# A quarter of the weights' low parts computed on GpSimd instead of VectorE, in a seven-phase transformer kernel

## The chip, the cores and the metric

The kernel runs on one core of one Trainium2 chip. The metric is the device time of one execution in microseconds (us), the median of three runs. The engines are called as the profile calls them: PE (TensorE, matmuls) with PEld (its weight loads), DVE (VectorE), ACT (ScalarE), POOL (GpSimd), SP (SyncE, which here only issues DMAs).

## What is computed

Two blocks run one after the other on x of 256 tokens by 1024 features, all in float32. The first has two layers: RMS norm, a projection to q, k, v and a gate, rotary embedding, attention (a sliding window with sinks in layer a, causal attention in layer b), the gate, an output projection, a residual. The second has two layers of a hybrid mixer (attention and a Mamba-2 scan side by side) and a SwiGLU:

```python
h = h + hybrid_mixer(rmsnorm_2(h, norm_mix[layer]), w_in[layer], ...)
h = h + swiglu(rmsnorm_2(h, norm_ffn[layer]), w_gate[layer], w_up[layer], w_down[layer])
...
def swiglu(h, w_gate, w_up, w_down):
    return (jax.nn.silu(h @ w_gate) * (h @ w_up)) @ w_down
```

Every weight matrix is read once from HBM: 140 MB in all.

## The kernel before

**Phases.** The names of tiles begin with the phase: `a`, `b` (the attention layers' projections), `m` (the mixers, twice), `f` (the SwiGLU's gate and up projections, twice), and with an `o` behind (`ao`, `bo`, `mo`, `fo`) the output projection of each. In the traced execution the matmuls of a run about from 3 to 81 us, ao to 107, b to 179, bo to 209, the first m to 316, mo to 355, the first f to 478, fo to 539, the second m to 643, mo to 680, f to 800, fo to the end.

**Three products for one.** A float32 product is made of three matmuls in the faster type fp32r. Each weight tile of 128 x 512 (two k tiles of 256 columns) is taken apart in `feed` (L362): `hi` is the raw weight rounded to fp32r, a copy on ACT or DVE (L392 to L395), and `lo` is `raw - hi`, a subtraction on DVE (L396). The activations are split likewise into `xh` and `xl`. `emit_slot` (L423) then issues hi by xh, hi by xl and lo by xh into one PSUM bank; in f the first two are one matmul of 512 columns. So each `lo` is needed by PE a little behind its `hi`. A sum of 526 such subtractions stands on DVE.

**The order is fixed when the program is built.** Each engine has its own queue, in order, and an instruction waits on semaphores for what it reads and for the buffer that it writes. The order in the queues comes from a planner within the kernel: `account` (L251) keeps for every engine a clock `clk` of when it would be done, `cost` (L223) gives the ns that an instruction is put down for, and `run_plan` (L487) calls in turn `feed` (next weights), `step_sides` (all that is not a weight matmul: attention, scan, norms, gates, each a chain that is resumed when PE's clock passes the end of its last step) and `emit_slot` (the next k tile's matmuls). `feed` runs ahead of PE by at most 60 k tiles (LEAD), and only while neither DVE's nor ACT's clock is over 500 ns ahead of PE's (AHEAD), unless the tile is needed within 5 (URGENT). It chooses the engine of the `hi` copy by the two clocks (L392). Other places choose by them too: `scaled` (ACT or DVE, whichever would be done first) and `spare`.

**Buffers.** Raw weights land by DMA from SP's queue in three buffers of 8 k tiles (`wraw`, RAW) or in pages; a buffer is loaded anew when its last `hi` and `lo` are done. `hi` and `lo` are pages of a pool of 64.

**POOL before.** It runs twelve powers of -1/2 of 128 x 2 numbers (the norms' reciprocal roots, in `columns` and `final`) and a few small fills, each put down at 650 ns by the planner.

Of the kernel before, what the change touches and what calls it, by code (L numbers as in the profile page):

```python
# [11 lines left out]
F32 = mybir.dt.float32  # L12
# [52 lines left out]
class Engine:  # L65


    def __init__(self, build, name, real):
        self.build, self.ename, self.real = build, name, real
# [43 lines left out]
class Build:  # L113
# [38 lines left out]
    def __init__(self, ctx, tc, io):  # L152
        self.tc = tc
        self.nc = Engines(self, tc.nc)
        self.clk = dict(PE=0.0, DVE=0.0, ACT=0.0, POOL=0.0)
        self.cur = Chain(None, 0.0)
        self.cur.start = 0.0
        self.count = 0
        self.io = io
        self.n = 0  # L160
        self.phase = "i"

        def pool(name, bufs, **kw):
            return ctx.enter_context(tc.tile_pool(name=name, bufs=bufs, **kw))

        self.cp = pool("const", 1)
        self.wraw = pool("wraw", self.RAW)
        self.fp = pool("f", self.PAGES)
        self.xp = pool("x", 4)
        self.up = pool("u", 2)  # L170
        self.hp = pool("h", 6)
        self.sp = pool("s", 8)
        psum = dict(space=bass.MemoryType.PSUM)
        self.pp = pool("psum", 8, **psum)
        self.banks = [0.0] * 8
        self.used = dict(mm=0, sc=0, tr=0, pv=0, out=0)
        self.sides = []
        self.ups = self.raws = 0
        self.planned = {}
        self.landing = 0.0  # L180
        self.live = self.wlive = self.most = 0
        self.kept = {}
        self.x = Timed(self)
        self.res = Timed(self)
        self.plan = []
        self.dma_i = self.cast_i = self.cast_k = self.cast_slot = 0
        self.seg_i = self.seg_k = self.seg_m = self.slot = 0
        self.dma_at = 1200.0
        self.queue = self.nc.sync
        self.units = {}  # L190
        self.bubbles = {}


    def name(self, s):
# [28 lines left out]
    def cost(self, eng, op, args, kw):  # L223
        out = kw.get("out", args[0] if args else None)
        aps = [x for x in list(args) + list(kw.values()) if hasattr(x, "shape")]
        n = 1
        for d in out.shape[1:]:
            n *= d
        cols = sum(1 for x in aps if x is not out and len(x.shape) == 2 and x.shape[1] == 1 and n > 1)
        psum = any("PSUM" in str(getattr(getattr(x, "tensor", x), "space", "")) for x in aps)  # L230
        if eng == "PE":
            if op == "transpose":
                return 110.0
            f32 = args[1].dtype == F32
            if args[1].dtype == BF16:
                return 69.0 if n == 128 else n / 2.4 * 1.02
            if f32 and out.shape[0] == 64:
                return 0.95 * n
            if n < 128:
                return 110.0 * (2 if f32 else 1)  # L240
            return n / 2.4 * (4 if f32 else 1) * 1.02
        if eng == "ACT":
            acc = "accum_out" in kw
            return (52.0 if psum else 93.0) + 0.833 * n + 93.0 * cols
        if eng == "POOL":
            return 650.0
        if op in ("tensor_copy", "tensor_scalar") and not psum:
            return 68.0 + 0.52 * n + 93.0 * cols
        return (130.0 if psum else 68.0) + 1.042 * n + 93.0 * (cols if op != "tensor_tensor_reduce" else 0)
# [112 lines left out]
    def feed(self):  # L362

        nc = self.nc
        while self.dma_i < len(self.plan) and self.raws < self.RAW:
            self.feed_dma()
        while self.cast_i < self.dma_i and self.cast_slot < self.slot + self.LEAD:
            now = self.clk["PE"]
            urgent = self.cast_slot < self.slot + self.URGENT
            if not urgent and max(self.clk["DVE"], self.clk["ACT"]) > now + self.AHEAD:  # L370
                return
            s = self.plan[self.cast_i]
            if s["at"] > now:
                self.landing = s["at"]
                return
            k = s["k0"] + self.cast_k
            n = min(2, s["k1"] - k)
            if self.wlive >= self.WMIN and self.wlive + self.live + self.SPARE > self.PAGES:
                return
            self.wlive += 2  # L380
            raw = s["raw"][:, self.cast_k:self.cast_k + n, :]
            hi = self.fp.tile([P, n, S], F32R, tag="f", name=self.name("hi"))
            if s["mode"] == "dt":

                both = hi[:, :, 0:32]
                raw, hi, lo = raw[:, :, 0:16], both[:, :, 0:16], both[:, :, 16:32]
            else:
                lo = self.fp.tile([P, n, S], F32R, tag="f", name=self.name("lo"))
            at = s["at"]
            self.cur = Chain(None, at)  # L390
            self.cur.start = at
            if self.clk["DVE"] + self.SWAP < self.clk["ACT"]:  # L392
                nc.vector.tensor_copy(hi, raw)
            else:
                nc.scalar.activation(hi, raw, AF.Copy)  # L395
            nc.vector.tensor_sub(lo, raw, hi.bitcast(F32))  # L396
            for i in range(n):
                s["parts"][k + i] = ((both if s["mode"] == "dt" else hi)[:, i, :], lo[:, i, :], self.cur.ready)
            self.cast_k += n
            self.cast_slot += n  # L400
            if s["k0"] + self.cast_k == s["k1"]:
                self.cast_i += 1
                self.cast_k = 0
                if s["page"]:
                    self.drop()
                else:
                    self.raws -= 1
# [1317 lines left out]
```

## Time and profile before

| | |
|---|---|
| median of 3 runs | 883.34 us (882.36 to 884.08) |
| the profiled execution | 882.25 us |
| its span, from first to last instruction | 880.2 us |
| busy: PE, DVE, ACT, POOL | 865.3, 731.8, 556.8, 14.6 us |
| matmuls recorded | 6451 |
| read from HBM | 140.15 MB |
| PE's granted clock, mean | 0.997 of full speed |

The profile is of one execution. "Busy" is the time in which at least one instruction of an engine was under way; matmuls overlap, so a busy PE is not PE at its peak. The times in the views count from the span's start.

### The profile page before, as it was taken

To read this page: it belongs to the slowest core of one execution; us is meant where nothing else is said; L and a number is where in the kernel's file an instruction comes from. 1 tells how busy PE (TensorE), PEld (TensorE's weight loads), DVE (VectorE), ACT (ScalarE), POOL (GpSimd) and SP (SyncE) were. 2 spreads that over 40 slices of the span, in tenths; PEclk is the share of its full clock that TensorE was granted. 3 is DMA by queue.
4 is the path that set the end of the run, shared out by engine and by line. 5 is a ranking of instruction groups with operands and counts; after the bars stand their busy time and mean duration, and the time that the engine had idled before them with its cause. 6 is when DMAs were issued, how large, how long until landed. Compare 5 with 4: busy or idle time off the path is not lost.

```text
span 880.2 us, 16862 instructions
## 1 busy us (share of the span) xinstructions
PE 865.3 (98%) x6451; PEld 793.9 (90%) x6451; DVE 731.8 (83%) x1652; ACT 556.8 (63%) x1325; POOL 14.6 (2%) x30
## 2 busy tenths in 40 slices
PE   8999999999999999999999999999999999999996
PEld 7987999889999789888888889999899888889996
DVE  6999899998899998899988668889878898998431
ACT  6378763677688885666666445579655666666321
POOL 0000010000000000000000000000000000000000
PEclk9999999999999999999999999999999999999998
DMA  8512673035543046666655637420046665665401
GB/s 315 206 74 73 225 275 130 26 107 177 199 145 108 26 132 215 200 226 224 234 207 179 234 127 274 158 73 25 2 137 217 224 229 200 240 220 187 167 1 48
DMA packets 30385, 142.30 MB, mean 162 GB/s; under 512 B 5344, under 2 KB 6880, under 8 KB 18400
## 3 DMA queue, kind: packets, MB, share of 16 engines
q1 hardware_dynamic: 30016, 141.08, 46.8%
q8 instruction: 51, 0.84, 0.4%
q14 instruction: 30, 0.25, 0.1%
q10 hardware_dynamic: 288, 0.14, 0.1%
HBM read 140.15 MB, written 1.05 MB: 160 GB/s over the span
## 4 chain that ended last, share of the span: by engine, by line
PE 66%; issue 21%; DVE 6%; ACT 4%; DMA 2%; SPq 0%; POOL 0%; POOLq 0%; DVEq 0%
PE m__p L78 20%; PE f__p L78 15%; PE mo__p L78 9%; PE b__p L78 8%; PE fo__p L78 7%; PE bo__p L78 3%; PE ao__p L78 3%; PE a__p L78 1%; DVE a__lo L78 1%; DVE a__sm L78 1%; ACT m__m L78 1%; DMA cst<-cst 1%; DMA fo__raw<-wa 1%; DVE a__pe L78 1%; DVE a__rope L78 1%
## 5 line engine op out<-in xcount | busy, mean ns | idle before, releaser
L78 PE MATMUL f__p<-mo__x,f__hi 128*128 128x512 f32 x492 | 174.6, 396 | 0.0
L78 DVE TENSOR_TENSOR f__lo<-f__raw,f__hi 128x512 fp32r<-128x512 f32 x186 | 123.0, 687 | 21.7 <-ACT f__hi L78 21.1
L78 PE MATMUL f__p<-mo__x,f__lo 128*128 128x256 f32 x492 | 138.0, 280 | 0.0
L78 PEld LDWEIGHTS f__p<-mo__x,f__hi 128*128 128x128 f32 x492 | 92.3, 188 | 21.5
L78 ACT ACTIVATE f__hi<-f__raw 128x512 fp32r<-128x512 f32 x186 | 104.6, 621 | 0.0
L78 PEld LDWEIGHTS f__p<-mo__x,f__lo 128*128 128x128 f32 x492 | 93.0, 189 | 0.0
L78 PE MATMUL fo__p<-f__r,fo__hi 128*128 128x256 f32 (+1 forms) x308 | 74.1, 322 | 0.0
L78 ACT ACTIVATE f__sum<-f__p 128x256 f32<-128x256 f32 x84 | 29.8, 383 | 56.8 <-PE f__p L78 56.7
L78 PE MATMUL f__p<-f__x,f__hi 128*128 128x512 f32 x176 | 63.6, 395 | 0.0
L78 DVE TENSOR_TENSOR m__lo<-m__raw,m__hi 128x512 fp32r<-128x512 f32 x74 | 50.2, 687 | 11.8 <-ACT m__hi L78 11.1
L78 PE MATMUL fo__p<-f__r,fo__lo 128*128 128x256 f32 x208 | 58.5, 281 | 0.0
L78 PEld LDWEIGHTS fo__p<-f__r,fo__hi 128*128 128x128 f32 x308 | 51.4, 190 | 4.4
L78 PE MATMUL m__p<-bo__x,m__hi 128*128 128x256 f32 (+1 forms) x292 | 54.2, 287 | 0.5 <-ACT m__m L78 0.5
L78 PE MATMUL mo__p<-mo__r,mo__hi 128*128 128x256 f32 x288 | 52.5, 284 | 0.0
L78 PE MATMUL a__p<-fo__x,a__hi 128*128 128x256 f32 x272 | 50.8, 287 | 0.7 <-ACT a__hi L78 0.7
L78 PE MATMUL f__p<-f__x,f__lo 128*128 128x256 f32 x176 | 49.3, 280 | 0.0
L78 DVE TENSOR_TENSOR fo__lo<-fo__raw,fo__hi 128x512 fp32r<-128x512 f32 (+1 forms) x60 | 37.3, 669 | 11.9 <-ACT fo__hi L78 9.3
L78 PEld LDWEIGHTS m__p<-bo__x,m__hi 128*128 128x128 f32 (+1 forms) x292 | 44.8, 188 | 2.4 <-issue 1.3
L78 PEld LDWEIGHTS mo__p<-mo__r,mo__hi 128*128 128x128 f32 x288 | 44.8, 192 | 0.2 <-issue 0.2
L78 ACT ACTIVATE m__hi<-m__raw 128x512 fp32r<-128x512 f32 x66 | 40.0, 635 | 7.3 <-DMA m__raw<-w 7.3
L78 PEld LDWEIGHTS a__p<-fo__x,a__hi 128*128 128x128 f32 x272 | 42.1, 191 | 2.1 <-ACT a__hi L78 1.3
L78 ACT ACTIVATE fo__hi<-fo__raw 128x512 fp32r<-128x512 f32 (+2 forms) x61 | 31.7, 580 | 17.4 <-DMA fo__raw<-w 10.0
(540 smaller groups left out, 2465.0 us busy)
## 6 DMA issues: line engine op xcount, KB each, us to landing
f__raw<-wu SPq DMA_DIRECT2D x20, 1024.0 KB, 4.8
f__raw<-wg SPq DMA_DIRECT2D x19, 1024.0 KB, 4.8
m__raw<-w SPq DMA_DIRECT2D x17, 1024.0 KB, 4.8
f__raw<-wd SPq DMA_DIRECT2D x9, 1024.0 KB, 4.9
b__raw<-wb SPq DMA_DIRECT2D x7, 1024.0 KB, 6.4
fo__raw<-wd SPq DMA_DIRECT2D x7, 1024.0 KB, 4.9
mo__raw<-wo SPq DMA_DIRECT2D x12, 512.0 KB, 3.7
fo__raw<-w SPq DMA_DIRECT2D x5, 1024.0 KB, 4.9
```

The lines of the kernel that those rows point to most:

```text
L78: return fn(*args, **kw)
```

## The change

In `feed`, the subtraction that makes `lo` may now go to POOL. The planner works out when DVE and when POOL would finish it, from the later of the engine's clock and the time when the `hi` copy is done, and takes POOL where that is no later than DVE (never for the small tiles of mode "dt"). `cost` puts down a POOL instruction of 64 elements or more at 100 + 2.3 ns for each element, 1278 ns for the usual 512. `share` only counts.

```diff
@@ -243,7 +244,7 @@
         if eng == "POOL":
-            return 650.0
+            return 650.0 if n < 64 else 100.0 + 2.3 * n
...
@@ -393,7 +394,12 @@
             else:
                 nc.scalar.activation(hi, raw, AF.Copy)
-            nc.vector.tensor_sub(lo, raw, hi.bitcast(F32))
+
+            t = max(t for t in self.cur.last.values())
+            late = [max(t, self.clk[e]) + self.cost(e, "tensor_sub", (lo, raw), {}) for e in ("DVE", "POOL")]
+            sub = nc.gpsimd if late[1] <= late[0] and s["mode"] != "dt" else nc.vector
+            sub.tensor_sub(lo, raw, hi.bitcast(F32))
+            self.share[sub is nc.gpsimd] += 1
```

In the built program 132 of the 526 subtractions stand on POOL: 12 in a (one of them half as long), 3 in ao, 17 in b, 2 in bo, 13 and 6 in the two m, 4 and 5 in the two mo, 30 and 31 in the two f, 6 and 3 in the two fo. Since the planner's clocks now run differently, its other choices move too: 11 `hi` copies, 23 scalings and taps of the mixers and the attention go from ACT to DVE (DVE has 34 such instructions more and 4 additions of 512 elements less, ACT 46 less). PE has as many instructions as before, interleaved a little differently.

The first place is POOL's queue around the norm of layer b. The rows are `lo` subtractions and the powers, `b__s<-b__s,mhalf`. Before:

```order
L78 TENSOR_TENSOR a__s_387<-a__s_385,mhalf 128x2
L78 TENSOR_TENSOR b__s_1773<-b__s_1771,mhalf 128x2
L78 TENSOR_TENSOR m__s_3310<-m__s_3308,mhalf 128x2
L78 TENSOR_TENSOR m__s_3346<-m__s_3306,mhalf 128x2
L78 MEMSET m__u_3424 128x2x3
```

Now:

```order
L78 TENSOR_TENSOR b__lo_1709<-ao__raw_1557,b__hi_1708 128x512
L78 TENSOR_TENSOR b__lo_1713<-ao__raw_1557,b__hi_1712 128x512
L78 TENSOR_TENSOR b__lo_1773<-ao__raw_1590,b__hi_1772 128x512
L78 TENSOR_TENSOR b__lo_1781<-ao__raw_1633,b__hi_1780 128x512
L78 TENSOR_TENSOR b__s_1805<-b__s_1803,mhalf 128x2
L78 TENSOR_TENSOR b__lo_1921<-b__raw_1797,b__hi_1920 128x512
L78 TENSOR_TENSOR b__lo_1973<-b__raw_1823,b__hi_1972 128x512
```

The norm's power stands behind four subtractions of the same phase; before, it had nothing but the last norm's power ahead of it.

The second place is DVE's queue late in the second f, twelve rows up to the product of a unit with its gate (`f__sum<-f__p` adds the two halves of a PSUM bank, `f__rowh` and `f__row` are the norm's factors, `f__gt` the gate). Before:

```order
L78 TENSOR_TENSOR f__lo_10594<-f__raw_10463,f__hi_10593 128x512
L78 TENSOR_TENSOR f__lo_10605<-f__raw_10463,f__hi_10604 128x512
L78 SCALAR_TENSOR_TENSOR f__gt_10575<-f__gt_10575,f__sum_10544 128x512
L78 TENSOR_TENSOR f__lo_10621<-f__raw_10463,f__hi_10620 128x512
L78 TENSOR_TENSOR f__sum_10609<-f__p_10533,f__sum_10609 128x256
L78 TENSOR_TENSOR f__sum_10609<-f__p_10534,f__sum_10609 128x256
L78 TENSOR_TENSOR f__lo_10637<-f__raw_10514,f__hi_10636 128x512
L78 TENSOR_TENSOR f__lo_10645<-f__raw_10514,f__hi_10644 128x512
L78 TENSOR_TENSOR f__sum_10609<-f__sum_10609,f__row_9574 128x512
L78 TENSOR_TENSOR f__lo_10658<-f__raw_10514,f__hi_10657 128x512
L78 TENSOR_TENSOR f__lo_10668<-f__raw_10514,f__hi_10667 128x512
L78 TENSOR_TENSOR f__sum_10609<-f__sum_10609,f__gt_10575 128x512
```

Now, up to the same step:

```order
L78 TENSOR_TENSOR f__sum_10666<-f__p_10597,f__sum_10666 128x256
L78 TENSOR_TENSOR f__sum_10666<-f__p_10598,f__sum_10666 128x256
L78 TENSOR_TENSOR f__sum_10666<-f__sum_10666,f__rowh_9568 128x512
L78 SCALAR_TENSOR_TENSOR f__gt_10679<-f__gt_10679,f__sum_10666 128x512
L78 TENSOR_TENSOR f__lo_10700<-f__raw_10500,f__hi_10699 128x512
L78 TENSOR_TENSOR f__lo_10714<-f__raw_10574,f__hi_10713 128x512
L78 CAST f__hi_10730<-f__raw_10574 128x512
L78 TENSOR_TENSOR f__lo_10731<-f__raw_10574,f__hi_10730 128x512
L78 TENSOR_TENSOR f__sum_10723<-f__p_10660,f__sum_10723 128x256
L78 TENSOR_TENSOR f__sum_10723<-f__p_10661,f__sum_10723 128x256
L78 TENSOR_TENSOR f__sum_10723<-f__sum_10723,f__row_9566 128x512
L78 TENSOR_TENSOR f__sum_10723<-f__sum_10723,f__gt_10679 128x512
```

POOL's queue about there:

```order
L78 TENSOR_TENSOR f__lo_10566<-f__raw_10363,f__hi_10565 128x512
L78 TENSOR_TENSOR f__lo_10626<-f__raw_10426,f__hi_10625 128x512
L78 TENSOR_TENSOR f__lo_10686<-f__raw_10500,f__hi_10685 128x512
L78 TENSOR_TENSOR f__lo_10746<-f__raw_10574,f__hi_10745 128x512
L78 TENSOR_TENSOR f__lo_10806<-f__raw_10634,f__hi_10805 128x512
```

Of seven subtractions in twelve rows of DVE three are left, beside a `hi` copy that has come from ACT; the unit's own additions and products stand closer together, and POOL does a subtraction or two for every four `lo` that a raw buffer of 8 k tiles gives.

## Rows read from the trace of the kernel before

**Rows 1.** The page, part 1: busy time of each engine, its share of the span, instructions.

```profile
PE 865.3 (98%) x6451; PEld 793.9 (90%) x6451; DVE 731.8 (83%) x1652; ACT 556.8 (63%) x1325; POOL 14.6 (2%) x30
```

**Rows 2.** Busy time of each engine in nine stretches of the span.

```profile
core 0: us, PE busy (x) PEld busy (x) DVE busy (x) ACT busy (x) POOL busy (x), PEclk, DMA share, GB/s
...
0.00:20.00 20.00, 15.99 (x111) 13.89 (x111) 11.37 (x26) 13.06 (x30) 0.34 (x6) 1.00 0.86 306
...
33.00:81.00 48.00, 47.10 (x394) 40.88 (x392) 46.99 (x154) 30.80 (x104) 0.00 (x0) 1.00 0.25 89
...
107.00:179.00 72.00, 72.00 (x607) 67.37 (x605) 66.44 (x182) 41.41 (x102) 2.79 (x1) 1.00 0.41 143
...
209.00:268.00 59.00, 59.00 (x493) 58.63 (x492) 53.65 (x125) 40.85 (x90) 2.19 (x8) 1.00 0.53 180
...
268.00:316.00 48.00, 46.69 (x418) 40.60 (x418) 45.06 (x121) 44.70 (x145) 0.00 (x0) 1.00 0.18 56
...
355.00:478.00 123.00, 123.00 (x714) 108.40 (x713) 110.37 (x212) 79.34 (x173) 0.69 (x1) 1.00 0.62 216
...
680.00:800.00 120.00, 120.00 (x685) 104.18 (x684) 109.30 (x200) 77.80 (x161) 1.07 (x1) 1.00 0.64 221
...
800.00:880.00 80.00, 72.33 (x589) 71.10 (x587) 31.66 (x54) 26.15 (x51) 0.69 (x1) 0.97 0.26 90
```

**Rows 3.** Chain of work that ended last, in order of time: its longest piece.

```profile
691.80 181.25 issue
```

**Rows 4.** Timeline, DVE and PE: first low part of a stage, and its first matmul.

```profile
107.19 0.69 DVE L78 TENSOR_TENSOR b__lo<-ao__raw,b__hi 128x512 fp32r<-128x512 f32 x1
...
114.32 0.28 PE L78 MATMUL b__p<-b__x,b__lo 128*128 128x256 f32 x1
...
355.89 0.69 DVE L78 TENSOR_TENSOR f__lo<-mo__raw,f__hi 128x512 fp32r<-128x512 f32 x1 [0.63 <-ACT f__hi L78]
...
362.18 0.28 PE L78 MATMUL f__p<-f__x,f__lo 128*128 128x256 f32 x1
...
682.33 0.68 DVE L78 TENSOR_TENSOR f__lo<-mo__raw,f__hi 128x512 fp32r<-128x512 f32 x1
...
686.17 0.28 PE L78 MATMUL f__p<-mo__x,f__lo 128*128 128x256 f32 x1
```

**Rows 5.** Timeline of DVE beside three powers on GpSimd, and a CAST: start, length.

```profile
115.64 2.49 DVE L78 TENSOR_TENSOR b__lo<-b__raw,b__hi 128x512 fp32r<-128x512 f32 x4
...
221.02 1.89 DVE L78 TENSOR_TENSOR m__lo<-m__raw,m__hi 128x512 fp32r<-128x512 f32 x3
...
365.17 0.75 DVE L78 TENSOR_TENSOR f__sum<-f__p,f__sum 128x256 f32<-128x256 f32 x2
...
599.91 0.42 DVE L78 CAST m__hi<-m__raw 128x512 fp32r<-128x512 f32 x1
```

**Rows 6.** Timeline of GpSimd (POOL): four of its twelve powers.

```profile
115.90 2.79 POOL L78 TENSOR_TENSOR b__s<-b__s,mhalf 128x2 f32<-128x2 f32 x1 [91.00 <-ACT b__hi L78]
...
221.25 1.00 POOL L78 TENSOR_TENSOR m__s<-m__s,mhalf 128x2 f32<-128x2 f32 x1 [102.57 <-DVE m__s L78]
...
223.55 0.69 POOL L78 TENSOR_TENSOR m__s<-m__s,mhalf 128x2 f32<-128x2 f32 x1 [1.30 <-PE m__p L78]
...
365.33 0.69 POOL L78 TENSOR_TENSOR f__s<-f__s,mhalf 128x2 f32<-128x2 f32 x1 [30.73 <-DVE f__s L78]
```

**Rows 7.** Busy time of instructions on PSUM tiles alone; columns of rows 2 without POOL.

```profile
33.00:81.00 48.00, 43.35 (x362) 37.95 (x360) 18.58 (x42) 5.74 (x12) 1.00 0.25 89
...
209.00:268.00 59.00, 58.91 (x490) 58.63 (x491) 8.32 (x20) 1.73 (x4) 1.00 0.53 180
...
268.00:316.00 48.00, 41.84 (x379) 34.52 (x346) 13.10 (x32) 19.47 (x70) 1.00 0.18 56
...
355.00:478.00 123.00, 123.00 (x712) 108.27 (x711) 16.48 (x45) 14.71 (x42) 1.00 0.62 216
```

More of the change, by code (lines that the diff above doesn't have):

```diff
@@ L191, in __init__ @@
         self.bubbles = {}
+        self.share = [0, 0]
     def name(self, s):
```

## The prediction

> **What bounds the kernel.** I read the busy times of the page first: PE is busy for 865.3 us of a span of 880.2, DVE for 731.8, POOL for 14.6 [rows 1]. So all that another engine could give back is 14.9 us. The same by stages shows where they lie [rows 2]: 4.0 us in the first 20 (loads; PE has 15.99), 7.7 in the last 80 (the tail behind the last matmul; 72.33), hence 3.2 in all the rest. Of these, 0.9 are in 33 to 81, where DVE is busy for 46.99 of 48 us and sets the pace, and 1.3 in 268 to 316, where DVE (45.06) and ACT (44.70) take turns. In b (107 to 179) and both f (355 to 478, 680 to 800) PE is busy throughout, though DVE is at 90% there. The chain of waits says it from the other side: its longest piece, 181.25 us from 691.80 on, is PE's own issue with no wait for anyone [rows 3]. The change does not touch PE's work: as many matmuls, as many columns. **It can give 3.2 us at most, and the question is what it can cost.**
>
> A cost needs the low parts to come late. How early they come now, the first subtraction of a stage and the first matmul that reads it show [rows 4]: in b it ends at 107.19 + 0.69 = 107.88, its matmul starts at 114.32, a lead of 6.4 us; in the first f 356.58 against 362.18, 5.6; in the second f 683.01 against 686.17, 3.2. These leads are all that stands between a slower DVE and PE.
>
> **What is removed.** 132 subtractions leave DVE. Four in a row take 2.49 us and one 0.69 [rows 4, 5], so each holds the queue for (2.49 - 0.69) / 3 = 0.60 us: 79 us less on DVE. On the other side the planner, which sees DVE lighter, gives it 34 copies and scalings more and 4 additions less; at 0.42 us (a CAST [rows 5]) and 0.69 that is 34 x 0.42 - 4 x 0.69 = 11.5 us, of which I count 2.5 in each f (six copies) and 4 in the first m. ACT sheds 46 instructions; it is the bound nowhere but between 268 and 316, so I give that nothing.
>
> **What is added, and its two unknowns.** POOL gets 132 subtractions of 512 elements. No row shows one. Its shortest instruction with two inputs, a power of two elements, takes 0.69 us, the longest 2.79 [rows 6]; those are the bounds of the time. I take 1.28, the planner's own figure for 512 elements in the diff, about twice what DVE needs.
>
> The second unknown is what DVE does meanwhile, and here the trace speaks. The same power takes 0.69 us at 223.55, when DVE does nothing, and 0.69 at 365.33, when DVE adds from a PSUM bank (`f__sum<-f__p`). It takes 1.00 at 221.25 beside DVE's subtractions, and 2.79 at 115.90: it ended at 118.69, so its 0.69 us began at 118.0, when the four subtractions that DVE had begun at 115.64 were done [rows 5, 6]. POOL waits while DVE works from SBUF alone, and not while DVE reads PSUM. The POOL instructions of before read next to nothing, so no row shows the reverse; I take it that the way is held by whoever came first, that a POOL subtraction holds it for all its 1.28 us, and that DVE's SBUF work stands still. The bounds are 0 (DVE feels nothing) and 2.79 us.
>
> [...]
>
> So a moved subtraction costs DVE q x 1.28 - 0.60 us, where q is the share of DVE's time without PSUM. From DVE's time on PSUM tiles and from its busy time by stage [rows 2, 7] q is 1 - 18.58 / 46.99 = 0.60 in 33 to 81, 1 - (8.32 + 13.10) / (53.65 + 45.06) = 0.78 in the first m (209 to 316), 1 - 16.48 / 110.37 = 0.85 in f. For the first 33 us and b I take 0.78.
>
> - **a**: five of its twelve go in the first 33 us, 5 x 0.40 = 2.0 us, seven after, 7 x 0.17 = 1.2. DVE has nothing spare there: **+3**.
> - **b**: 17 x 0.40 and four copies at 0.42 are 8.5 us on top of 66.44 in a stage of 72. 2.9 too many, but the lead is 6.4: **0**. POOL's queue now has subtractions ahead of the norm's power. That it came 2.1 us late at 115.90 cost PE nothing (72.00 of 72), and one more wait of 1.28 I put at 0 too.
> - **first m**: 13 x 0.40 + 4 = 9.2 on top of 98.71 in 107: 0.9 too many, **+1**.
> - **first f**: 30 x 0.49 + 2.5 = 17.2 on top of 110.37: 127.6 in a stage of 123. Over by 4.6, with a lead of 5.6, which DVE's waits for PE and ACT use up in part: **+1.5**.
> - **second f**: 31 x 0.49 + 2.5 = 17.7 on top of 109.30: 127.0 in 120. Over by 7.0, lead 3.2; part of the work is for the next stage and may come late: **+3**.
> - ao, bo, both mo, the second m and both fo have 29 between them, and more room: **0**. DMAs: SP's next load into a raw buffer waits for POOL's subtraction as it did for DVE's; there are three buffers, and the transfers keep their lead as long as the `lo` keep theirs, so 0.
>
> Sum: 3 + 1 + 1.5 + 3 = 8.5 us on the profiled execution's 882.25, 890.8. The median of the runs is 1.1 above that execution, so **892**.
>
> [...]
>
> **The rivals.** Under 0.2% (1.8 us) a measurement of this kernel can't tell a change from none.
>
> - *The leads swallow all.* DVE is over its stages only by what the buffered leads hold, and a's 3 us shrink since PE there lacks 0.9. For: the overrun in the first f is smaller than its lead. Against: the second f. It gives 883.3, within 0.2%.
> - *DVE feels nothing* (or POOL's hold is under 0.60 / 0.78 = 0.77 us, from where each moved subtraction relieves DVE). It turns the sign: DVE loses 12 x 0.60 = 7.2 us in a, where it sets the pace, 7.8 in the first m, and PE fills its 3.2 us there. For: no row shows DVE waiting for POOL. Against: POOL waits for DVE, and one way for two engines is most simply exclusive. 882.25 - 3.2 + 1.1 = 880.2, faster.
> - *Each change of hands costs as well.* The power of 1.00 us shows 0.31 of waiting beside running subtractions; if DVE loses that much on top, the hold is 1.59 and a moved subtraction costs 0.75 in f. First f 135.4 in 123, less the lead, 6.8; second f 135.1 in 120, 11.9; first m 4.5; a 5.7: 29 in all, 912.
>
> That the change does not do what it says is no case: the queues as built hold the 132.
>
> **How the numbers follow.** Chances: forecast 0.44, leads swallow all 0.22, DVE feels nothing 0.23, changes of hands 0.11. The forecast's own range is 886 to 901 (one stage's term doubled, or the f terms gone). Over all cases I say 879 to 906: it takes in the gain of 3 us with one more for the interleaving, and leaves out the last rival and a little of the rest. Faster by over 0.2%: the third case less a bit whose gain is under 1.8 us, 0.22. Slower: forecast and last rival, 0.55. Within: 0.23.
>
> **What would show it.** Right: DVE's SBUF instructions beside a POOL subtraction take up to 1.3 us longer or begin that much later, PSUM ones do not; POOL's subtractions take 1.1 to 1.4 us when alone; the leads at the end of f are gone, and PE's idle time before `lo` matmuls in a and the second f names POOL or DVE. Wrong: DVE's subtractions keep 0.69 us beside POOL's, or DVE's total busy time falls by some 68 us (79 less 11.5) while PE's idle time is as before.

## The result and the profile after

| | before | after |
|---|---|---|
| median of 5 runs | 882.78 us (882.36 to 884.08) | 927.53 us (920.84 to 928.72) |
| the profiled execution, its span | 882.25, 880.2 us | 920.84, 919.1 us |
| PE's granted clock, mean | 0.997 | 0.987 |

The ratio is 1.049 (1.046 to 1.052): 44.7 us slower, outside the range of 879 to 906. The profiled execution is the fastest of the five; the other four have a mean granted clock of 0.978 to 0.983.

Part 1 of the page of after, the answer to [rows 1]:

```profile
PE 878.2 (96%) x6451; PEld 801.4 (87%) x6451; DVE 773.6 (84%) x1550; ACT 538.1 (59%) x1279; POOL 206.5 (22%) x162
```

DVE has 102 instructions fewer and is busy 41.8 us longer. Where that comes from is in the groups by line, shape and tile of after (count, busy us, mean ns):

```profile
L78 DVE TENSOR_TENSOR f__lo<-f__raw,f__hi 128x512 fp32r<-128x512 f32 x122 | 99.0, 838 | 3.1 <-ACT f__hi L78 0.7 <-PE f__p L78 0.5
L78 DVE TENSOR_TENSOR f__sum<-f__p,f__sum 128x256 f32<-128x256 f32 x84 | 31.4, 414 | 0.0
L78 DVE TENSOR_TENSOR f__sum<-f__sum,f__rowh 128x512 f32<-128x512 f32 x22 | 30.0, 1364 | 0.4
```

Before, their means were 687, 417 and 685 ns. What reads a PSUM bank (`f__p`) is as it was, what works from SBUF alone takes longer, the product with `f__rowh` twice as long. The timelines of POOL and of DVE in one place of the first f show why (start, length):

```profile
442.44 1.30 POOL L78 TENSOR_TENSOR f__lo<-f__raw,f__hi 128x512 fp32r<-128x512 f32 x1 [3.40 <-ACT f__hi L78]
...
442.63 1.66 DVE L78 TENSOR_TENSOR f__lo<-f__raw,f__hi 128x512 fp32r<-128x512 f32 x1
444.21 0.41 DVE L78 TENSOR_TENSOR f__sum<-f__p,f__sum 128x256 f32<-128x256 f32 x1
```

DVE's subtraction starts 0.19 us behind POOL's and ends at 444.29, 0.55 us after POOL's end at 443.74. It takes 0.97 us longer than its usual 0.69, and most of those 0.69 lie behind POOL's end: it stood still until POOL was done. Of the 1177 DVE instructions that touch no PSUM tile (names in `__p`) 117 are over 0.1 us longer than the median of their operation and shape before, together 105.0 us, the longest by 1.14; of the 373 that touch one, none. So the hold is 105.0 / 132 = 0.80 us for each moved subtraction. Below, "hold" is such stretch of DVE's instructions, in sum; the runs without GpSimd's subtractions give it as a difference of DVE's busy time too.

The low parts do not come late. The answer to [rows 4] in b, timelines of DVE and PE:

```profile
113.64 0.69 DVE L78 TENSOR_TENSOR b__lo<-ao__raw,b__hi 128x512 fp32r<-128x512 f32 x1
...
131.87 0.28 PE L78 MATMUL b__p<-ao__x,b__lo 128*128 128x256 f32 x1
```

The lead is 131.87 - 114.33 = 17.5 us; it was 6.4. In the two f the first `lo` and the first matmul that reads one are (timelines of POOL, DVE and PE):

```profile
376.52 1.75 POOL L78 TENSOR_TENSOR f__lo<-mo__raw,f__hi 128x512 fp32r<-128x512 f32 x1
...
389.55 0.28 PE L78 MATMUL f__p<-f__x,f__lo 128*128 128x256 f32 x1
...
713.98 0.69 DVE L78 TENSOR_TENSOR f__lo<-mo__raw,f__hi 128x512 fp32r<-128x512 f32 x1 [0.63 <-ACT f__hi L78]
...
722.79 0.28 PE L78 MATMUL f__p<-mo__x,f__lo 128*128 128x256 f32 x1
```

These leads are 11.3 us (before 5.6) and 8.1 us (before 3.2). PE waits for DVE's other steps. All its waits in the trace come to 33.4 us, before to 7.7, and none of after's is put down to a `hi` or a `lo`. The 25.7 us more of waits and PE's busy time, 12.9 us longer, make up nearly all of the 38.9 us by which the span grew. The two longest waits are for a rotary product in b and for the last residual. Timelines of PE, of DVE, and of PE again:

```profile
166.07 0.28 PE L78 MATMUL b__p<-ao__x,b__lo 128*128 128x256 f32 x1
171.02 1.22 PE L78 MATMUL b__p<-b__rope,b__rope 64*128 64x128 f32 x6 [4.66 <-DVE b__rope L78]
...
169.20 1.76 DVE L78 TENSOR_TENSOR b__rope<-b__rope,b__rot 128x512 f32<-128x512 f32 x1
...
861.38 1.30 PE L78 MATMUL fo__p<-cst,fo__hg 128*128 128x128 f32 x4 [4.38 <-ACT fo__hg L78]
```

What PE was late for at 861.38 the chain of waits follows back, in order of time (start, length):

```profile
846.15 0.69 DVE f__lo L78
846.83 0.35 DVE fo__hi L78
847.21 1.72 DVE fo__lo L78
848.92 0.68 DVE fo__sum L78 x2
849.62 0.70 DVE fo__sum L78
850.35 0.70 DVE fo__sum L78
...
851.13 0.64 ACT fo__r L78
851.79 0.55 DVE fo__r L78
...
852.40 0.69 DVE fo__lo L78
...
853.15 5.08 DMA fo__raw<-wd
...
858.31 0.64 ACT fo__hi L78
858.98 0.69 DVE fo__lo L78
859.67 0.61 DVE fo__h L78
860.30 0.63 ACT fo__sq L78
860.93 0.41 ACT fo__hg L78
```

DVE is behind; its `fo__lo` of 852.40 frees a raw buffer late, the load into it lands at 858.23, and the residual `fo__h`, which does not need that weight, stands in DVE's queue behind the `lo` that does. The chain into the rotary product of 171.02 runs through late loads as well, each behind a `lo` of DVE:

```profile
125.85 0.61 DVE b__lo L78
...
126.51 6.55 DMA b__raw<-wb
...
149.04 1.21 DVE b__lo L78 x2
150.27 4.74 DMA b__raw<-wo
```

For the whole span the chain is now PE 49%, DVE 29%, DMA 8% (before PE 66%, DVE 6%, DMA 2%).

PE's granted clock is lower too. Three stretches of after, the last inside the first (columns of [rows 2]):

```profile
160.00:180.00 20.00, 15.34 (x111) 13.88 (x110) 19.48 (x53) 6.79 (x17) 4.05 (x3) 0.83 0.28 96
846.00:866.00 20.00, 13.63 (x96) 12.77 (x96) 16.78 (x27) 11.21 (x22) 2.55 (x2) 0.91 0.68 230
...
169.00:175.00 6.00, 3.98 (x19) 3.33 (x20) 6.00 (x9) 2.77 (x4) 3.08 (x2) 0.50 0.21 78
```

DVE is busy for 19.48 of the 20 us around the wait in b. Within that wait the clock falls: from 168.6 on PE is granted 0.50, for 6.8 us.

### The profile page after: what moved, and what is told of

Its sections match the earlier page's. It is cut to its first block, busy times and chain, and to the rows that moved or that the text cites. A ratio compares the mean times of both kernels' runs of the same rounds, so it can differ in the third digit from the quotient of the medians.

```text
span 919.1 us, 17113 instructions
## 1 busy us (share of the span) xinstructions
PE 878.2 (96%) x6451; PEld 801.4 (87%) x6451; DVE 773.6 (84%) x1550; ACT 538.1 (59%) x1279; POOL 206.5 (22%) x162
## 4 chain that ended last, share of the span: by engine, by line
PE 49%; DVE 29%; DMA 8%; issue 8%; ACT 6%; SPq 0%; POOL 0%; DVEq 0%; POOLq 0%; ACTq 0%
PE f__p L78 19%; PE m__p L78 16%; PE fo__p L78 6%; DVE f__sum L78 3%; DVE f__lo L78 3%; PE bo__p L78 3%; PE b__p L78 3%; DVE mo__lo L78 2%; PE a__p L78 2%; DVE b__lo L78 1%; DVE m__xs L78 1%; DVE m__lo L78 1%; DMA mo__raw<-wg 1%; DMA mo__raw<-wo 1%; DVE a__lo L78 1%
## 5 line engine op out<-in xcount | busy, mean ns | idle before, releaser
L78 PE MATMUL f__p<-mo__x,f__hi 128*128 128x512 f32 x400 | 142.2, 396 | 0.0
L78 PE MATMUL f__p<-mo__x,f__lo 128*128 128x256 f32 x400 | 112.2, 281 | 0.0
L78 POOL TENSOR_TENSOR f__lo<-f__raw,f__hi 128x512 fp32r<-128x512 f32 x54 | 75.1, 1397 | 163.8 <-ACT f__hi L78 114.1
L78 DVE TENSOR_TENSOR f__lo<-f__raw,f__hi 128x512 fp32r<-128x512 f32 x122 | 99.0, 838 | 3.1 <-ACT f__hi L78 0.7
L78 PE MATMUL f__p<-f__x,f__hi 128*128 128x512 f32 x244 | 87.0, 393 | 0.0
L78 PE MATMUL f__p<-f__x,f__lo 128*128 128x256 f32 x244 | 68.4, 280 | 0.0
L78 PEld LDWEIGHTS f__p<-f__x,f__hi 128*128 128x128 f32 x244 | 45.7, 187 | 10.5
L78 PEld LDWEIGHTS f__p<-f__x,f__lo 128*128 128x128 f32 x244 | 46.1, 189 | 0.0
L78 DVE TENSOR_TENSOR fo__lo<-fo__raw,fo__hi 128x512 fp32r<-128x512 f32 (+1 forms) x49 | 31.7, 692 | 15.8 <-ACT fo__hi L78 12.9
L78 PE MATMUL fo__p<-f__r,f__hi 128*128 128x256 f32 (+1 forms) x180 | 43.8, 326 | 0.0
L78 DVE TENSOR_TENSOR m__lo<-m__raw,m__hi 128x512 fp32r<-128x512 f32 x48 | 32.5, 688 | 11.0 <-ACT m__hi L78 10.6
```

The costliest lines, as they stand in the source:

```text
L78: return fn(*args, **kw)
```

## The experiments

In every diff `tc.nc` issues without telling the planner (unbooked), `nc` books; `MOVED` is a constant with a bit for each subtraction that the change puts on GpSimd, `moved()` in these cuts a test of it. "Place" is one of these 132. All times are medians; the kernel before ran beside them at 882.1 to 882.6.

**1. What holds DVE.** The order of before, and at the places GpSimd work that nobody needs. (A copy reads `raw` alone, so it starts when the load lands and not, as a subtraction does, when `hi` is done.)

```diff
             nc.vector.tensor_sub(lo, raw, hi.bitcast(F32))
+            if moved():
+                tc.nc.gpsimd.tensor_sub(junk, raw, hi)       # e2
+                tc.nc.gpsimd.tensor_sub(tiny, raw[:, 0, 0:2], hi[:, 0, 0:2])   # e3
+                tc.nc.gpsimd.memset(junk, ...)               # e3, twice
+                tc.nc.gpsimd.tensor_copy(junk, raw)          # e8
```

> The order of the kernel before with all subtractions on DVE; at the 132 places GpSimd repeats the subtraction into a scratch tile that nobody reads, and the planner does not know of it. Nothing waits for GpSimd's results. Theory (a GpSimd subtraction holds DVE's SBUF work by 0.8 us on average): DVE busy 731.8 + about 100 = 830 us, and more loss than the change since nothing leaves DVE: 930 to 980 us. If the change's loss came of its order or of GpSimd's results coming late: 883, DVE busy 732.

> As the run before it, but at the 132 places GpSimd does a subtraction of two elements (which only keeps the place in time) and two fills of 128 x 512, which write SBUF and read nothing. It tells what of a GpSimd instruction holds DVE. If only reading from SBUF holds: DVE's subtractions keep 0.69 us, DVE busy 732 to 760, 883 to 890 us. If any use of SBUF by GpSimd holds, writes too: DVE busy over 800 and a loss as with the repeated subtractions, in proportion to the fills' length (a fill's length no trace shows).

> The order of the kernel before, all subtractions on DVE; at the 132 places GpSimd copies raw (128x512, one input) into a scratch tile, unbooked. It tells whether GpSimd's reading from SBUF with one input holds DVE as the subtraction with two did (841 us busy on DVE, 950 us), or not, as the fills did (734, 884). If any reading holds, in proportion to the copy's length (no row shows it; by the fill at least 0.53 us): DVE busy 780 to 840 us and 915 to 950 us. If only two inputs hold: 883 to 886.

Measured: subtractions 950.09 us, DVE busy 841.1; fills 883.81, DVE 734.2; copies 882.77, DVE 759.3. DVE's subtractions in f, and POOL's work beside them, from the groups by line and shape; with subtractions:

```profile
L78 DVE TENSOR_TENSOR f__lo<-f__raw,f__hi 128x512 fp32r<-128x512 f32 x186 | 147.2, 816 | 10.1 <-ACT f__hi L78 9.0
```

With fills:

```profile
L405 POOL MEMSET junk<- 128x512 f32 x132 | 70.0, 530 | 7.6
...
L78 DVE TENSOR_TENSOR f__lo<-f__raw,f__hi 128x512 fp32r<-128x512 f32 x186 | 123.0, 686 | 22.6 <-ACT f__hi L78 21.6
```

With copies:

```profile
L78 DVE TENSOR_TENSOR f__lo<-f__raw,f__hi 128x512 fp32r<-128x512 f32 x186 | 131.8, 734 | 8.3 <-ACT f__hi L78 7.6
```

So GpSimd's reading holds DVE's subtractions (816 ns beside subtractions, 734 beside copies) and its writing does not: fills leave 686 ns, where before has 687, although there are 264 of 0.53 us. A copy (0.64 us at 444.81 in e8, with one input) holds for 27.5 / 132 = 0.21 us, a subtraction (1.29 us alone) for 109.3 / 132 = 0.83 us; how much of the difference comes of the copies' other start is not shown.

Fills do hold a few other DVE instructions, with one input of full size: in their run 12 TENSOR_SCALAR and one CAST are 0.14 to 0.48 us longer than the median before, 4.0 us in all. Timelines of DVE and of POOL:

```profile
295.70 0.85 DVE L78 CAST m__hi<-m__raw 128x512 fp32r<-128x512 f32 x1
...
295.75 0.52 POOL L405 MEMSET junk<- 128x512 f32 x1
```

Two things were unexpected. The copies' 27.5 us on DVE cost nothing (expected 915 to 950 if reading holds): where they fall, the order of before has that much to spare. And the subtractions' 109.3 us cost 67.7.

**2. The change without its hold.** The order of the change, its 132 `lo` filled instead (`FILLED` stands for the condition of each run, here always true):

```diff
-            sub.tensor_sub(lo, raw, hi.bitcast(F32))
+            if sub is nc.gpsimd and FILLED:
+                self.account("POOL", "tensor_sub", (lo, raw, hi), {})
+                tc.nc.gpsimd.tensor_sub(tiny, raw[:, 0, 0:2], hi[:, 0, 0:2])
+                tc.nc.gpsimd.memset(lo, 0.0)
+                tc.nc.gpsimd.memset(lo, 0.0)
+            else:
+                sub.tensor_sub(lo, raw, hi.bitcast(F32))
```

> The changed kernel with its order, but GpSimd fills each of its 132 lo tiles with zeros (two fills, together about 1.06 us, behind a subtraction of two elements that waits for hi) in place of subtracting: the low parts of a quarter of the weights are left out, and with them the hold on DVE, since fills did not hold it. DVE's 102 us of stretch go, DVE busy about 672 us. Theory (the loss is the hold): 879 to 884 us, PE's waits for x splits, sums and r gone. If the new order, or lo coming over GpSimd, costs by itself: 900 to 927.

Measured: **878.72 us**, ratio 0.996 (0.994 to 0.998), DVE busy 677.1. This settles the cause: order, GpSimd's latency and everything else of the change are faster by 3.7 us (1.6 to 5.0) than before; PE lacked 3.2. All of the loss, 927.5 - 878.7 = 48.8 us, comes with the hold, of which the fills leave 4.5 us. The traced execution, 882.09 us, is one of three of ten without the gain, so no trace shows where it arises. The run leaves work out, so it is a bound, no better version.

**3. Where the hold costs.** The same with `FILLED` everywhere but in one group of stages (`share[1]` below 34; 34 to 50 and 87 to 97; the rest), and in every second place (`share[1] % 2`):

> The changed kernel's order; GpSimd subtracts only the first 34 lo (a, ao, b, bo) and fills its other 98 with zeros (those low parts are left out), so the hold stands in the attention layers alone. The prediction's terms: 3 us in these stages: about 882 (no hold at all 878.7). If the two traces are read rightly (these stages end 14.7 us later than without any hold): 892 to 896.

> As the run before it, with the 28 subtractions of the mixers (m, mo, both) real and the other 104 filled with zeros. The prediction's term: 1 us, about 880. By the traces (these stages take 8.2 and 3.2 us more than without any hold, part of it the lag that the stages ahead leave): 884 to 890.

> As the two before it, with the 70 subtractions of the SwiGLU stages (f, fo, both) real and the other 62 filled with zeros. The prediction's term: 4.5 us, about 883. By the traces (the two take 1.1 and 12.1 us more than without any hold): 890 to 896, with most of it at the end of the second, where PE waits for a late transfer.

> The changed kernel's order; every second of the 132 is subtracted on GpSimd, the others are filled with zeros (the low parts of an eighth of the weights are left out). So about half the hold, 51 us. Theory of slack (an order forgives some tens of us of DVE time above its plan, then each is one us of span; with no hold this order took 878.7, with 102 us 927.5): 879 to 888, most of the loss gone. If each hold costs by itself what it is long where it falls (linear): 903.

| hold in | places | us | over no hold | the prediction's term |
|---|---|---|---|---|
| a, ao, b, bo | 34 | 898.33 | 19.6 | 3 |
| m, mo | 28 | 894.65 | 15.9 | 1 |
| f, fo | 70 | 897.70 | 19.0 | 4.5 |
| every second place | 66 | 892.89 | 14.2 | |
| all (the change) | 132 | 927.53 | 48.8 | 8.5 |

The three groups sum to 54.5, near the whole: each loses its own, and hardly any is caught up in the next. A hold in a to bo or in the mixers costs 0.57 us of the span, in f and fo 0.27. Half the holds, spread evenly, cost 29% of the loss, between the two expectations. So evenly spread holds are cheap at first, while the ones gathered in a to bo or in the mixers are not. The three stage runs came out higher than the traces had let me expect, by 2 to 5 us each (the trace of after is of its fastest execution).

**4. The same DVE time in other forms.** DVE's own subtractions in place of GpSimd's hold, and a part of the hold:

```diff
             sub.tensor_sub(lo, raw, hi.bitcast(F32))
+            # e1: where sub is GpSimd, booked there, issued as tc.nc.vector.tensor_sub(lo, raw, hi)
+            # e11: behind each fill of part 2, twice:
+            tc.nc.vector.tensor_sub(junk, raw[:, 0, :], hi[:, 0, :])
...
             nc.vector.tensor_sub(lo, raw, hi.bitcast(F32))
+            if moved():
+                tc.nc.vector.tensor_sub(junk, raw[:, 0, :], hi[:, 0, :])       # e6
+                tc.nc.gpsimd.tensor_sub(junk, raw, hi)       # e10, at 51 of the places
```

The first piece is on the change (e1, e11), the second on the kernel before.

> The change's order to the row, but the 132 subtractions are issued to DVE at the place where they stood for GpSimd; the planner still books them on GpSimd. No GpSimd work, so no hold; DVE gets 132 x 0.60 = 79 us that no clock counts. Theory (unbooked time on DVE makes PE wait for DVE's steps; in the changed kernel it was the hold, 102 us in the trace): about 79 / 102 of the change's loss of 45 us, so 35: 910 to 925 us, PE waiting for the x splits, the sums and r, not for lo. If the new order alone costs: 927. If the loss needs GpSimd (its slow or late subtractions): 883 to 890.

> The order of the kernel before, GpSimd idle; at the 132 places DVE does a subtraction of half the width (128x256, about 0.35 us) more, into scratch, and the planner does not know of it: 132 x 0.35 = 46 us more on DVE, about what the change adds to DVE's busy time (41.8). If the change costs what it adds to DVE, wherever it comes from: 920 to 930. If it is the single stops of a microsecond at steps that PE waits for, rather than DVE's total, these small pieces cost less: 890 to 905.

> The order of the kernel before, all subtractions on DVE, and 51 of the 132 repeated on GpSimd into scratch, unbooked: 51 x 0.83 = 42 us of hold, DVE busy about 774, as in the run with 132 half-width subtractions on DVE (773.4 us, 893.2). If only the sum of DVE's time above the plan counts: 890 to 897. If a stop of a microsecond at one step costs PE more than small pieces of the same sum: 900 to 910.

> The changed kernel's order with GpSimd's 132 lo filled with zeros (left out, no hold), and behind each of them two unbooked half-width subtractions on DVE into scratch: 264 x 0.34 = 90 us in place of the 102 us of hold; DVE busy 677 + 90 = 767. If the sum above the plan counts, whatever makes it: 910 to 922. If it needs GpSimd's stops: under 900.

| order of | extra on DVE | DVE busy | us |
|---|---|---|---|
| before | none | 731.8 | 882.4 |
| before | copies' hold (e8) | 759.3 | 882.8 |
| before | 51 holds (e10) | 770.9 | 888.6 |
| before | small subtractions (e6) | 773.4 | 893.2 |
| before | 132 holds (e2) | 841.1 | 950.1 |
| the change | none (e5) | 677.1 | 878.7 |
| the change | 66 holds (e9) | 719.2 | 892.9 |
| the change | its 132 on DVE (e1) | 746.8 | 900.3 |
| the change | small subtractions (e11) | 769.9 | 909.1 |
| the change | 132 holds (after) | 773.6 | 927.5 |

DVE's busy time is from the profiled execution, which in e9 (886.2 us) and after (920.8) is 7 us under the median.

At about the same 773 us on DVE the order of before takes 888.6 with holds and 893.2 with small pieces, the order of the change 927.5 and 909.1. It is not DVE's total that decides, but how far DVE is above what its order was made for, and in what form: the change's order takes 21.6 us more when DVE has 69.7 more than the planner knew (e1), without GpSimd's subtractions. I had expected 910 to 925 there, since I took the loss to go with that time in proportion to the holds'. DVE's own work costs less: 0.31 us for each us in e1, 0.33 in e11. For holds over all stages the price grows, from 0.34 (e9) to 0.51 (all). The run e11 multiplies the same zeros as e5, so they are not what makes e5 fast. That single stops of a microsecond cost more than small pieces fell in before's order (888.6, not 900 to 910), but not in the change's, where 92.8 us in pieces cost 30.4 and 96.5 of hold 48.8. By the profiled traces that difference lies behind the second mixer: from there to fo's last low-part matmul after takes 200.7 us, the run with pieces 188.7 (the two traces are 11 us apart, the medians 18). How much of that the last holds ahead of the late transfer make was tried with `FILLED` at four places (`share[1]` 126 to 129):

> The changed kernel, with four of GpSimd's 132 filled with zeros instead (left out): those that ran from 830 to 849 us, ahead of the transfer that lands at 858. If four holds there (some 4 us) make the raw buffer free late and with it the transfer, PE's 6.9 us of waits at 850 to 861 go, and the half clock behind them (1.7): 917 to 921. If DVE's lag there was built up over the whole second f: 924 to 927.

Measured: 922.73 us (919.96 to 924.85), with the four filled; after's executions overlap with that. By the traces the waits at 850 to 852 are gone, the one for `fo__hg` is still there, 3.5 us instead of 4.4. So part of DVE's lag there was built up earlier; between the two expectations. Why small pieces build up less lag than holds is open.

**5. A planner that knows.** The change with the same 132 on GpSimd, its planner charging DVE 780 ns for each; the same with fills; and the order of before with e6's work booked:

```diff
             sub.tensor_sub(lo, raw, hi.bitcast(F32))
+            if sub is nc.gpsimd:
+                self.clk["DVE"] = max(self.clk["DVE"], self.clk["POOL"] - 1278.0) + 780.0
```

> The changed kernel with the same 132 subtractions on GpSimd, but the planner adds 780 ns to DVE's clock for each, from the time when GpSimd's starts (102 us of stretch in the trace / 132). The order then follows from a DVE that is as slow as it is. Theory (the loss comes from the planner's not knowing of the hold; capacity is there): the hold stays, DVE busy about 770, but PE's waits for DVE's steps go: 885 to 900 us. If DVE plus hold is simply too much work for the span, or if GpSimd's results come late: 915 to 930 as the change.

> The order of the run whose planner charged DVE 780 ns for each GpSimd subtraction (898.8 us), with fills of zeros on GpSimd in place of the 132 (a quarter of the low parts left out, no hold). It tells what made its 16 us over the kernel before. If the order that the planner makes for a slower DVE is the worse one: 892 to 899. If the hold still falls elsewhere than planned: 879 to 886.

> As the run before it, but the planner books the 132 half subtractions on DVE's clock and orders around them. Theory (DVE has the capacity, the loss is from time that the planner does not know of): 883 to 895. If DVE is at its limit in too many stages, booked or not: as the unbooked one, 905 to 930.

Measured: charged 898.80, charged without hold 893.20, booked 901.80. Charging takes 28.7 of the 44.7 us away, and brings in another loss: with next to no hold its order still takes 11 us more than before. Between these two runs the hold is 749.8 - 660.2 = 89.6 us of DVE's busy time and costs 5.6 us: in an order that charges for it, and that loses 11 us anyway, it is nearly free. And some 42 us of DVE work cost more when the planner knows of them (901.8) than when not (893.2), between the two expectations. That knowing would suffice fell: told of a slower DVE, this planner orders worse. In these orders PE waits longest at the end of the first mixer (3.5, 3.5 and 3.2 us); which rule of the planner does it wasn't tried.

No version that does all the work beats the kernel before. A moved subtraction holds DVE for 0.80 us and relieves it of 0.60 [rows 5].

## Why the prediction was wrong

**The sign and the hold were right.** POOL's subtraction takes 1.29 us (1.28 taken). Beside it DVE's SBUF work stands still and its PSUM work does not: `f__lo` takes 838 ns on average, before 687, the additions from a PSUM bank 414 and 417. That the way is held by whoever came first, for the whole instruction, was my assumption; the runs show the 0.80 us on average. With next to no hold the time is 878.7, near the 880.2 of the rival by which DVE feels nothing. The norm's power behind four subtractions cost nothing, as taken: PE's waits for POOL in after are 0.2 us in all.

**DVE's added time was not the mistake.** q x 1.28 - 0.60 and the copies came to 55.8 us over a, b, m and both f; DVE got 41.8 over the whole span, since a hold is 0.80 us and not about 1.

**The step that failed is "A cost needs the low parts to come late".** From it came the leads as the measure of what is free. In after the leads are longer, 17.5 us instead of 6.4 in b, no wait of PE is for a `lo`, and the loss is 45. What PE waits for are steps that it needs with no lead at all: x splits, rotary products, softmax sums, the residual; a hold is paid there. That the planner, which takes DVE for lighter, lets `feed` run further ahead and so puts more low parts into DVE's queue ahead of these steps is argued from the leads and from the chain at 858; no run changed that alone. So every term was too small, by the table of part 3: 3 for 19.6 in the attention layers (b, ao and bo at 0), 1 for 15.9 in the mixers, 4.5 for 19.0.

**To charge a stage only for its overrun was the wrong test with it.** I charged only what went beyond a stage's length, so in b (66.44 busy of 72) and ao and bo nothing. But the 34 holds in a to bo, which put 700.3 - 677.1 = 23.2 us on DVE, cost 19.6 us of span. What DVE has idle within a stage did not take them up; that it is idle only between turns with ACT and PE is my reading, not shown.

**The order was costed as 34 operations on DVE.** It is also what DVE's time is measured against: the same 773 us, made by holds or pieces, cost 6 to 11 in one order and 27 to 45 in the other.

**The DMAs, put at 0, failed too.** The load of 853.15 is the case that I excluded, a raw buffer that comes free late; PE waits 4.4 us for what is queued behind it. The chain into the wait of 171.02 has two more. **The clock** was not in the sum at all.

Of the rivals the last came nearest with 912, but not by its mechanism: at 0.80 us the hold is shorter than the subtraction, not longer by 0.31. (By its own numbers its first m is 4.0, not 4.5; the sum stays near 912.) That the leads swallow all is refuted by the leads themselves.

## What to carry to other kernels

An order that is fixed in advance may have a little slack (in the order of before the copies' 27.5 us on DVE cost nothing) or none where the holds gather (in the order of the change 23.2 us in a to bo cost 19.6), and there a microsecond that it wasn't made for cost 0.8 of the span: cost a slower engine against what its order assumes, and look for the steps that the next engine needs at once, not for the ones that have a lead. Before moving work from VectorE to GpSimd, compare what the move relieves with what GpSimd's reading holds (0.60 against 0.80 us here), and measure the move with fills in its place: that run tells in one number what the rest of the change is worth. A planner's price for an engine must hold what that engine does to others, and still the order that it then makes has to be measured.

## What the runs showed of the hardware

The granted clock: within or behind waits of PE of 1.4 to 4.7 us the record shows 0.50 in four stretches of after that before doesn't have, from 124.2 (3.4 us), 168.6 (6.8), 240.3 (3.4) and 861.5 (3.4). It is not so at every wait: behind 2.3 us before 384.83 it stays at 1.00. Three matmuls of b in a row take 0.64 us from 173.40 on, at 0.50, and 0.36 from 164.39 on, at 1.00; by estimate from these the 17 us cost up to 17.0 x 0.28 / 0.64 = 7.4, a fifth of the profiled execution's loss. The other four executions have a lower mean clock and are 6 to 8 us longer; no trace shows whether it is by more such stretches. In before, 169 to 175 is at 1.00, and the only such stretch is at the end, 7.7 us from 874.8; after has that one too.

GpSimd's times on 128x512 float32, alone: fill 0.53 us (e3), copy 0.64 (e8), subtraction 1.29 (after). The subtraction takes about twice the copy's time, but holds DVE four times as long (0.83 us in e2 against 0.21 in e8). The longest single holds there are 1.13 and 0.46 us; the copies hold 77 instructions of DVE, the subtractions 123.
